# Hymba decoder layer on one Trainium2 core: the q, k, v projection shifted by 0.18 of a head pair against the attention that it runs beside, and the SSD half of the output projection begun later, with its evictions moved from VectorE to ScalarE and GpSimd

## The chip, the cores and the metric

One core of a Trainium2 chip runs the whole layer in one launch. The metric is the device time in microseconds (us). TensorE (PE) multiplies, with its weight loads on a queue of their own (PEld); VectorE (DVE), ScalarE (ACT) and GpSimd (POOL) do everything else; SyncE (SP) issues almost all DMAs, in one queue.

## The reference, cut to what matters

One layer on 1024 tokens of width 1024. The first sub-layer projects the normed input once, gives the first part to a Mamba-2 SSD mixer (16 heads) and the last 3072 columns to a stick-breaking attention (16 heads of 64), and projects both outputs back together:

```
q = rms_norm(q per head, q_norm_w); k = rms_norm(k per head, k_norm_w)
for each block of 128 queries:
    logits = q_blk @ k.T / 8                 # keys up to the block's end
    rem    = where(s < t, 1 - sigmoid(logits), 1)
    weights = where(s < t, sigmoid(logits) * (product of rem over the later keys), 0)
    out_blk = weights @ v
y = concat(norm(y_ssd), attention) ;  x1 = x + gate * (y @ w_out)
x2 = x1 + gate2 * swiglu(norm(x1))          # afterwards
```

The reference writes the product as an exponential of a cumulative sum of logarithms; the kernel forms it directly with a scan. `y_ssd` is normed in two groups of 512 columns, each with a factor of its own per token (`yr` in the kernel), which the kernel applies after the matmul to each group's product.

## The kernel before, in words

Every product is of float32 quality: both operands are split into a high and a low part, and `mm3` issues three matmuls (high·high, high·low, low·high) for each logical one.

Heads go in eight pairs, p = 0 to 7. The part of the program that the change touches is one list of "atoms": pieces of work, each with a time in units of one pair's attention. The list is sorted by that time, and the atoms are issued in this order. PE's instructions run in exactly this order; on the other engines a scheduler at build time sets the order. Four kinds of atoms matter:

- *Attention of pair p* (`Step`, lines 818 to 885), times p to p + 1: four steps i, each of two query blocks (0 and 1, 2 and 3, up to 7). A block n has (n + 1) x 128 keys. PE computes the logits `pl`, ACT takes two sigmoids of them (lines 843, 844), DVE runs the scan (line 848) and the multiplication (line 850) over the block's whole width for each of two heads, PE transposes the weights (`ptw`), ACT copies them out (line 865), and PE sums (`pa`). So the scans grow from 128 to 1024 columns in a pair and start again at 128.
- *Projection of pair p + 1*, beside the attention of pair p (`qkv_unit`, `unit_atoms`): four units u of 256 tokens, each 48 matmuls of 128x384 (`pp`), copied out by ACT (lines 777, 778). A norm follows: ACT squares, DVE reduces (line 785), GpSimd takes a reciprocal square root in small operations (lines 118 to 129, tile `rs_y`), DVE multiplies (line 790). Then PE transposes q and k (`pq`), ACT and DVE write their halves (lines 804 to 808). The attention of the next pair needs all this.
- *Weight pages.* The projection's weights of one pair are eight pages `wp` in nine buffers. During the last unit (u = 3), as each page is used for the last time, the page of the next pair is split into its place: high part by GpSimd (line 692), low part by DVE (line 694). I call the point between unit 3 of one pair and unit 0 of the next the border of the projection's pairs. With `SHIFT = 0` it coincides with the start of the next pair's attention.
- *The SSD half of the output projection* (`a0_block`), beside the attention of pair 7, which has no projection left to fill PE: eight blocks of 128 tokens, each with two groups of 12 matmuls of 128x384 (`poa`). Group 0 is evicted by ACT (line 984), group 1 by DVE (line 986), which adds group 0 in the same instruction. Two PSUM banks (pool `psp`) serve these accumulators. Input pages are loaded from DRAM (line 964) and split by ACT (968) and GpSimd (969). Line 671 sets when it begins (`A0T`) and how long a block takes (`A0D`). In the same stretch the weights of the next stage are loaded into seven buffers (line 1011) and split by ACT (1017) and DVE (1020). The next stage's matmuls are `po`.

Here pair 7's attention with all that lies beside it, up to the first `po`, is called the tail.

Of the kernel before, what the change touches and what calls it, by code (L numbers as in the profile page):

```python
# [10 lines left out]
AF = mybir.ActivationFunctionType  # L11
ALU = mybir.AluOpType
# [7 lines left out]
TB = S // P  # L20
# [9 lines left out]
def build(tc, t, dbg=None, stop=None):  # L30
    nc = tc.nc
# [635 lines left out]
    aw2 = ExitStack()  # L667
    apr = aw2.enter_context(tc.tile_pool(name="apr", bufs=1, side="right"))
    NP = H // 2
    SLOT0, CL, FL0, FL, FT0, LAG, LAGS, LAGQ, SHIFT, D0, E0, C0 = 300, 0.5, 0.0, 0.9, 0.12, 0.05, 0.1, 0.2, 0.0, 0.14, 0.0, -0.25  # L670
    A0T, A0D = 0.01, 0.14
    WD = -6
    WT = (7.18, 7.22, 7.26, 7.4, 7.7, 7.98, 7.99, 8.0)
    NPR, NWT = 3, 6
    CA = 3 * P
# [260 lines left out]
    def unit_atoms(p, u):  # L936

        g = qkv_unit(p, u)
        d = (NP - 1 + SHIFT) / (4 * (NP - 1))
        t0 = (4 * (p - 1) + u) * d  # L940
        if p == 0:
            d = D0
            t0 = (u - 4) * d + E0
        res = []
        for n in range(16):
            res.append((t0 + d * n / 16, lambda: next(g, None)))
            if u == 3 and p + 1 == NP and n < KT:
                res.append((t0 + d * (2 * n + WD) / 16, lambda n=n: qkv_load(NP, n)))
                res.append((t0 + d * (2 * n + 1) / 16 + 1e-6, lambda n=n: qkv_split(NP, n)))
            if u == 3 and p + 1 < NP:  # L950
                res.append((t0 + d * n / 16 + 1e-6, lambda n=n: qkv_weight(p + 1, n)))
        res.append((t0 + d + LAGS, lambda: next(g, None)))
        res.append((t0 + d + LAGQ, lambda: next(g, None), "unit"))
        return res


    x1 = [None] * TB
    y_pages, y_hl, x1_pages = [], {}, []

    def a0_load(i):  # L960
        if not y_pages:
            y_pages.extend(page("y_page").rearrange("p (k c) -> p k c", c=P) for _ in range(8))
            x1_pages.extend(apool.tile([P, D], F32, tag="page", name="x1") for _ in range(TB))
        dma(out=f32(y_pages[3 * (i & 1)]), in_=yssd_s[i])
# [7 lines left out]
    def a0_block(i):  # L972
        hi, lo = y_hl[i]
        x1[i] = x1_pages[i]
        xo = x1[i][:, 0:CA]
        for g in range(NG):
            po = psp.tile([P, 512], F32, tag="pp", name="poa")[:, 0:CA]
            for k in range(4 * g, 4 * g + 4):
                w = w_pages[NP, k]
                mm3(po, hi[:, k], lo[:, k], w[:, 0], w[:, 1], k == 4 * g, k == 4 * g + 3)  # L980
                if k % 4 < 3:
                    yield
            if g == 0:
                nc.scalar.activation(xo, po, AF.Copy, scale=yr[:, i:i + 1])
            else:
                nc.vector.scalar_tensor_tensor(out=xo, in0=po, scalar=yr[:, TB + i:TB + i + 1], in1=xo,
                                               op0=ALU.mult, op1=ALU.add)
            yield

    def a0_atoms():  # L990
        t0 = NP - 1 + A0T
        res = [(t0 - 0.01, lambda: a0_load(0)), (t0 - 0.01, lambda: a0_load(1)), (t0 - 0.005, lambda: a0_split(0))]
        for i in range(TB):
            t = t0 + i * A0D
            if i + 1 < TB:
                res.append((t + 0.1 * A0D, lambda i=i: a0_split(i + 1)))
            if i + 2 < TB:
                res.append((t + 0.2 * A0D, lambda i=i: a0_load(i + 2)))
            g = a0_block(i)
            for n in range(8):  # L1000
                res.append((t + A0D * n / 8, lambda g=g: next(g, None)))
        return res
# [22 lines left out]
    yr = rsqrt(NG * TB, yssq, 1.0 / 512, "yn", nc.gpsimd)  # L1025
# [427 lines left out]
    po = None  # L1453
# [45 lines left out]
```

## Time and profile before

| | us |
|---|---|
| time, median of 3 runs (lowest, highest) | 1788.65 (1782.85, 1790.51) |
| the profiled execution: its time, its span | 1781.2, 1779.5 |
| PE busy in the span | 1692.4 (95%) |
| DVE busy | 1190.8 (67%) |
| ACT busy | 839.9 (47%) |
| GpSimd busy | 298.0 (17%) |

The attention phase with the work beside it runs from about 402 to 947 us of the span. Of the page, in 40 slices of 44.5 us each, in tenths:

```
PE   3999999999999999999879999899999999999999
DVE  5597795757676676676786666976676666644541
PEclk9999999999999999999889999999999999999999
```

A digit is the busy share of a slice, in the third line the clock that TensorE was granted. The slices 9 to 20 (counted from 0) hold the attention phase: PE is at 9 tenths throughout, DVE at 6 to 8; only the last two (845 to 934 us) fall to 8 and 7 on PE, with a clock of 8 tenths: the tail.

### The profile page before, as it was taken

How to read it: one execution, taken by the hardware profiler on the slowest of the kernel's cores; microseconds unless marked ns; L12 is line 12 of the kernel's file. 1: busy time of each engine (PE TensorE's matmuls, PEld its weight loads, DVE VectorE, ACT ScalarE, POOL GpSimd, SP SyncE). 2: the span in 40 equal slices, each digit the busy share in tenths (PEclk: the TensorE clock that was granted, in tenths of full speed). 3: DMA queues.
4: the chain of work that ended last, by engine and by line, in shares of the span. 5: the costliest groups of instructions: out<-in, count | busy, mean ns of one | idle time of the engine just before them, and what ended most of it. 6: DMA issues, size and time to landing. Idle time of an engine off the chain costs nothing.

```text
span 1779.5 us, 24616 instructions
## 1 busy us (share of the span) xinstructions
PE 1692.4 (95%) x9025; PEld 1401.2 (79%) x9025; DVE 1190.8 (67%) x1789; ACT 839.9 (47%) x1651; POOL 298.0 (17%) x630
## 2 busy tenths in 40 slices
PE   3999999999999999999879999899999999999999
PEld 2777777798788778778669888688888888788887
DVE  5597795757676676676786666976676666644541
ACT  6545562556666566667564345533332332423220
POOL 2410001033422431432522710000000000000000
PEclk9999999999999999999889999999999999999999
DMA  8366355311101110111314433532332222844621
GB/s 282 117 220 209 119 181 155 105 54 43 42 21 34 45 37 16 45 42 30 118 38 143 160 119 111 149 125 78 95 113 77 87 86 72 274 158 148 236 89 48
DMA packets 175792, 192.17 MB, mean 108 GB/s; under 512 B 11560, under 2 KB 126516, under 8 KB 175671
## 3 DMA queue, kind: packets, MB, share of 16 engines
q1 hardware_dynamic: 174582, 190.07, 33.7%
q8 instruction: 71, 1.16, 0.3%
q10 hardware_dynamic: 1088, 0.52, 0.1%
q14 instruction: 51, 0.41, 0.1%
HBM read 155.88 MB, written 34.67 MB: 107 GB/s over the span
## 4 chain that ended last, share of the span: by engine, by line
PE 64%; DVE 14%; DMA 7%; issue 6%; ACT 4%; POOL 4%; SPq 1%; DVEq 0%; POOLq 0%; ACTq 0%
PE pdn L50 13%; PE pX L50 10%; PE pY L50 6%; PE pp L50 6%; PE po L50 6%; PE pZ L50 6%; PE px L50 5%; DVE pr L848 3%; PE pz L50 3%; PE pa L50 2%; DVE be L850 2%; PE pyd L50 2%; PE pl L50 1%; PE ptw L53 1%; DMA adaraw<-in_w_ada_dram 1%
## 5 line engine op out<-in xcount | busy, mean ns | idle before, releaser
L50 PE MATMUL pp<-wp,hh 128*128 128x384 f32 x1024 | 284.9, 356 | 14.5 <-DVE wp L694 13.3
L50 PE MATMUL pdn<-dw,ah 128*128 128x512 f32 x704 | 217.0, 389 | 1.5 <-DVE t L1334 1.5
L50 PEld LDWEIGHTS pp<-wp,hh 128*128 128x128 f32 x1024 | 173.5, 189 | 33.8 <-DVE wp L694 17.5
L848 DVE TENSOR_TENSOR_SCAN pr<-pr,idz 128x256 f32<-128x256 f32 (+7 forms) x128 | 175.5, 1392 | 29.2 <-ACT pr L843 29.2
L50 PE MATMUL pp<-wp,hl 128*128 128x384 f32 x512 | 172.7, 337 | 0.0
L50 PEld LDWEIGHTS pdn<-dw,ah 128*128 128x128 f32 x704 | 132.1, 188 | 29.4 <-DVE t L1334 2.0
L50 PE MATMUL pdn<-dw,al 128*128 128x512 f32 x352 | 136.9, 389 | 0.0
L843 ACT ACTIVATE pr<-pl 128x384 f32<-128x384 f32 (+3 forms) x192 | 97.2, 506 | 61.5 <-PE pl L50 44.9
L865 ACT COPY wt<-ptw 128x512 f32<-128x512 f32 (+1 forms) x160 | 88.8, 569 | 67.4 <-PE ptw L53 67.2
L1434 ACT CAST ah<-araw 128x1024 fp32r<-128x1024 f32 x44 | 46.4, 1055 | 142.9 <-PE pdn L50 130.6
L1298 ACT CAST wl<-s 128x512 fp32r<-128x512 f32 x88 | 54.8, 623 | 123.5 <-PE pX L50 42.0
L65 DVE TENSOR_TENSOR wl<-s,wl 128x512 fp32r<-128x512 f32 x88 | 60.6, 691 | 67.0 <-ACT wl L1298 66.3
L850 DVE TENSOR_TENSOR be<-be,pr 128x256 f32<-128x256 f32 (+7 forms) x128 | 101.8, 817 | 4.8
L790 DVE TENSOR_TENSOR qkraw<-qkraw,rs_y 128x256 f32<-128x256 f32 x64 | 34.3, 559 | 99.2 <-POOL rs_y L129 99.2
L844 ACT ACTIVATE be<-pl 128x384 f32<-128x384 f32 (+3 forms) x192 | 98.0, 510 | 0.1
L50 PEld LDWEIGHTS pp<-wp,hl 128*128 128x128 f32 x512 | 96.2, 188 | 0.2 <-issue 0.2
L65 DVE TENSOR_TENSOR al<-araw,ah 128x1024 fp32r<-128x1024 f32 x44 | 53.7, 1223 | 59.7 <-ACT ah L1434 59.6
L53 PE MATMUL ptw<-ident,be 128*128 128x128 f32 x576 | 90.6, 276 | 1.1 <-DVE be L850 1.1
L50 PE MATMUL pz<-zw,hh 128*128 128x512 f32 x256 | 89.5, 417 | 0.0
L1298 ACT CAST wl<-raw 128x512 fp32r<-128x512 f32 x62 | 38.5, 622 | 98.9 <-PE pY L50 41.6
L50 PE MATMUL pa<-wt,qv 128*64 128x256 f32 (+1 forms) x640 | 77.5, 374 | 4.0 <-ACT qv L778 3.8
L50 PE MATMUL po<-wb,yhi 128*128 128x512 f32 x256 | 80.9, 397 | 0.0
(373 smaller groups left out, 4055.2 us busy)
## 6 DMA issues: line engine op xcount, KB each, us to landing
araw<-a_s SPq DMA_DIRECT2D x44, 512.0 KB, 3.5
adaraw<-in_w_ada_dram SPq DMA_DIRECT2D x64, 256.0 KB, 3.4
wraw<-in_w_in_dram SPq DMA_DIRECT2D x64, 192.0 KB, 3.1
raw<-in_w_gate_dram SPq DMA_DIRECT2D x46, 256.0 KB, 3.0
raw<-in_w_up_dram SPq DMA_DIRECT2D x44, 256.0 KB, 3.2
draw<-in_w_down_dram SPq DMA_DIRECT2D x44, 256.0 KB, 3.4
ada_raw<-in_w_ada_dram SPq DMA_DIRECT2D x16, 512.0 KB, 5.9
seg<-csT_s SPq DMA_DIRECT2D x32, 256.0 KB, 3.1
```

The costliest lines, as they stand in the source:

```text
L50: link(nc.tensor.matmul(out, lhsT, rhs, start=start, stop=stop, skip_group_check=more))
L53: link(nc.tensor.transpose(out=out, in_=in_, identity=identity or ident))
L65: return nc.vector.tensor_tensor(out=lo, in0=src, in1=f32(hi), op=ALU.subtract)
L790: inst = nc.vector.tensor_tensor(out=r4[:, t2], in0=r4[:, t2], in1=r[:, t2].unsqueeze(2).to_broadcast([P, 4, HD]), op=ALU.mult)
L843: nc.scalar.activation(pr[:, c0:c1], pl[:, 0:c1 - c0], AF.Sigmoid, scale=-1.0)
L844: nc.scalar.activation(be[:, c0:c1], pl[:, 0:c1 - c0], AF.Sigmoid)
L848: nc.vector.tensor_tensor_scan(out=rev, data0=rev, data1=idz[:, S - n:][:, ::-1], initial=0.0, op0=ALU.mult, op1=ALU.max)
L850: nc.vector.tensor_tensor(out=be[:, 0:n], in0=be[:, 0:n], in1=pr[:, 1:n + 1], op=ALU.mult)
L865: nc.scalar.copy(wt[:, 0:m], pt[:, 0:m])
L1298: nc.scalar.copy(w[:, 0], src)
L1434: nc.scalar.copy(ah, raw)
```

## The change

`SHIFT` goes from 0 to 0.18: the projection of every pair is issued 0.18 of a pair later against the attention. Each unit lasts 0.25 of a pair, as before; only the first unit of pair 1 is stretched over the first 0.43 of pair 0's attention. The SSD half of the output projection begins at 7.27 instead of 7.01 and takes 0.1 instead of 0.14 per block; its first loads and its first split go to 7.18. Its second group is now evicted by ACT into the second 384 columns of the same page, `part`, and GpSimd adds that to the first.

```
-    ... SHIFT, D0, E0, C0 = ..., 0.0, 0.14, 0.0, -0.25
-    A0T, A0D = 0.01, 0.14
+    ... SHIFT, D0, E0, C0 = ..., 0.18, 0.14, 0.0, -0.25
+    A0T, A0D = 0.27, 0.1
 def unit_atoms(p, u):
-        d = (NP - 1 + SHIFT) / (4 * (NP - 1))
-        t0 = (4 * (p - 1) + u) * d
+        d = 0.25
+        t0 = SHIFT + (4 * (p - 1) + u) * d
+        if p == 1 and u == 0:
+            d, t0 = d + SHIFT, 0.0
 def a0_block(i):
-            if g == 0:
-                nc.scalar.activation(xo, po, AF.Copy, scale=yr[:, i:i + 1])
-            else:
-                nc.vector.scalar_tensor_tensor(out=xo, in0=po, scalar=yr[:, TB + i:TB + i + 1], in1=xo,
-                                               op0=ALU.mult, op1=ALU.add)
+            part = (xo, x1[i][:, CA:2 * CA])[g]
+            nc.scalar.activation(part, po, AF.Copy, scale=yr[:, g * TB + i:g * TB + i + 1])
+            if g:
+                nc.gpsimd.tensor_tensor(out=xo, in0=xo, in1=part, op=ALU.add)
 def a0_atoms():
-        t0 = NP - 1 + A0T
-        res = [(t0 - 0.01, lambda: a0_load(0)), (t0 - 0.01, lambda: a0_load(1)), (t0 - 0.005, lambda: a0_split(0))]
+        t0, t1 = NP - 1 + A0T, NP - 1 + SHIFT + 1e-3
+        res = [(t1, lambda: a0_load(0)), (t1, lambda: a0_load(1)), (t1 + 1e-3, lambda: a0_split(0))]
```

Later lines of the changed kernel have numbers higher by two (964 is 966, 1011 is 1013, 1017 is 1019); the evictions are lines 987 (ACT) and 989 (GpSimd).

Counted in PE's order: every pair from 1 to 6 keeps its 192 projection matmuls, pair 0 has 159 instead of 192 and four transposes fewer, and 33 matmuls and four transposes stand in pair 7 in their place.

On DVE, at the border of the projection's pairs, this is what stood before between the two halves of the widest block (`pr`, `be` are the scan and the multiplication, `wp` the low parts of the new pages, `qkred` the norm's reduction and `rs_y` the multiplication by the root):

```order
L785 TENSOR_REDUCE qkred<-sqv 128x8
L790 TENSOR_TENSOR qkraw<-qkraw,rs_y 128x256 x2
L848 SCALAR_TENSOR_TENSOR pr_3167<-pr_3167,idz 128x1024
L848 SCALAR_TENSOR_TENSOR pr_3165<-pr_3165,idz 128x1024
L850 TENSOR_TENSOR be<-be,pr_3167 128x1024
L850 TENSOR_TENSOR be<-be,pr_3165 128x1024
L694 SCALAR_TENSOR_TENSOR wp<-wraw,wp 128x384 x5
L808 SCALAR_TENSOR_TENSOR qv<-qkraw,cols_79,qv 128x256
L808 SCALAR_TENSOR_TENSOR kp<-qkraw,cols_79,kp 128x256
L694 SCALAR_TENSOR_TENSOR wp<-wraw,wp 128x384
```

And now on DVE, the same stretch and what follows it:

```order
L785 TENSOR_REDUCE qkred<-sqv 128x8
L790 TENSOR_TENSOR qkraw<-qkraw,rs_y 128x256 x2
L848 SCALAR_TENSOR_TENSOR pr_3165<-pr_3165,idz 128x1024
L848 SCALAR_TENSOR_TENSOR pr_3166<-pr_3166,idz 128x1024
L850 TENSOR_TENSOR be<-be,pr_3165 128x1024
L850 TENSOR_TENSOR be<-be,pr_3166 128x1024
L808 SCALAR_TENSOR_TENSOR qv<-qkraw,cols_79,qv 128x256
L808 SCALAR_TENSOR_TENSOR kp<-qkraw,cols_79,kp 128x256
L785 TENSOR_REDUCE qkred<-sqv 128x8
L790 TENSOR_TENSOR qkraw<-qkraw,rs_y 128x256 x2
L848 SCALAR_TENSOR_TENSOR pr_3167<-pr_3167,idz 128x128
L850 TENSOR_TENSOR be<-be,pr_3167 128x128
```

The new pages' splits have moved from behind the scans of 1024 columns to behind those of 128 columns of the next pair; a reduction with its multiplication stands there now. In a whole pair, all four reductions are now followed directly by the multiplication that needs GpSimd's root of it; before, two of four were not.

On DVE in the tail, before, the evictions of group 1 (`poa`) stood among the scans and multiplications of wide blocks:

```order
L986 SCALAR_TENSOR_TENSOR x_8945<-poa,rs_y,x_8945 128x384
L848 SCALAR_TENSOR_TENSOR pr_3165<-pr_3165,idz 128x640
L848 SCALAR_TENSOR_TENSOR pr_3166<-pr_3166,idz 128x640
L850 TENSOR_TENSOR be<-be,pr_3165 128x640
L850 TENSOR_TENSOR be<-be,pr_3166 128x640
L848 SCALAR_TENSOR_TENSOR pr_3167<-pr_3167,idz 128x768
L848 SCALAR_TENSOR_TENSOR pr_3165<-pr_3165,idz 128x768
L850 TENSOR_TENSOR be<-be,pr_3167 128x768
L850 TENSOR_TENSOR be<-be,pr_3165 128x768
L986 SCALAR_TENSOR_TENSOR x_8946<-poa,rs_y,x_8946 128x384
```

On ACT in the tail, now, the evictions of blocks 1 and 2 (both groups, line 987) stand among splits of the next stage's weights (`wa`):

```order
L1019 ACTIVATE wa<-waraw,cols_78 128x640
L987 ACTIVATE x_9009<-poa,rs_y 128x384
L1019 ACTIVATE wa<-waraw,cols_78 128x640
L865 COPY wt<-ptw 128x512
L1019 ACTIVATE wa<-waraw,cols_78 128x640
L987 ACTIVATE x_9009<-poa,rs_y 128x384
L1019 ACTIVATE wa<-waraw,cols_78 128x640
L865 COPY wt<-ptw 128x512
L987 ACTIVATE x_9010<-poa,rs_y 128x384
```

The evictions that waited among DVE's scans are gone from DVE; ACT's second to fourth ones now have a `wa` split ahead of each. On SP, the loads which these splits need are issued in this order now (`y_page` are the input pages of the SSD half, in the order of its blocks, `ysb_s` the attention's output):

```order
L883 DMA ysb_s<-yth 128x2x128
L966 DMA y_page<-yssd_s 128x1024 x2
L883 DMA ysb_s<-yth 128x2x128
L966 DMA y_page<-yssd_s 128x1024 x2
L1013 DMA waraw<-in_w_out_dram 128x640 x7
L966 DMA y_page<-yssd_s 128x1024 x2
L1013 DMA waraw<-in_w_out_dram 128x640
```

The seven weight loads stand behind the pages of blocks 4 and 5, as they did before; the pages themselves are loaded later.

## Rows read from the trace of the kernel before

**Rows 1.** Waits of PE, 310 to 960 us: total us, times, longest.
```profile
PE pp L50 <- DVE wp L694: 13.3, 11, 2.1
PE poa L50 <- DVE x L986: 8.7, 2, 7.8
PE poa L50 <- POOL y_page L969: 5.4, 1, 5.4
PE pa L50 <- ACT qv L778: 3.8, 6, 0.6
```
**Rows 2.** One pair's window: length, busy PE PEld DVE ACT POOL, PE's clock, DMA.
```profile
527.00:592.00 65.00, 62.15 (x435) 52.71 (x433) 45.74 (x61) 42.41 (x104) 20.89 (x65) 1.00 0.13 33
```
**Rows 3.** PE's timeline around a border: start, busy us, ..., [wait <-releaser].
```profile
490.82 1.15 PE L50 MATMUL pl<-kp,qv 64*128 64x256 f32 x12
...
505.57 1.49 PE L50 MATMUL pl<-kp,qv 64*128 64x384 f32 x12
509.13 0.60 PE L53 MATMUL pq<-ident,qkraw 128*128 128x128 f32 x4
...
522.70 0.60 PE L53 MATMUL pq<-ident,qkraw 128*128 128x128 f32 x4
...
529.96 0.44 PE L50 MATMUL pp<-wp,hh 128*128 128x384 f32 x1 [2.03 <-DVE wp L694]
```
**Rows 4.** The chain of waits, a run of projection matmuls: start, us.
```profile
388.96 4.70 PE pp L50 x27
```
**Rows 5.** DVE's timeline of the same pair.
```profile
493.12 2.87 DVE L848 TENSOR_TENSOR_SCAN pr<-pr,idz 128x640 f32<-128x640 f32 x2 [0.70 <-ACT pr L843]
497.36 0.48 DVE L808 SCALAR_TENSOR_TENSOR qv<-qkraw,cols,qv 128x256 fp32r<-128x256 f32 x1
498.15 0.68 DVE L785 TENSOR_REDUCE qkred<-sqv 128x8 f32<-128x512 f32 x1
...
502.84 0.76 DVE L790 TENSOR_TENSOR qkraw<-qkraw,rs_y 128x256 f32<-128x256 f32 x2 [4.01 <-POOL rs_y L129]
...
509.27 3.94 DVE L848 TENSOR_TENSOR_SCAN pr<-pr,idz 128x896 f32<-128x896 f32 x2 [0.64 <-ACT pr L843]
...
515.12 0.48 DVE L808 SCALAR_TENSOR_TENSOR qv<-qkraw,cols,qv 128x256 fp32r<-128x256 f32 x1
...
529.36 2.42 DVE L694 SCALAR_TENSOR_TENSOR wp<-wraw,wp 128x384 fp32r<-128x384 f32 x5
```
**Rows 6.** DVE's waits for the norm's root, 527 to 592 us: total, times, longest.
```profile
DVE qkraw L790 <- POOL rs_y L129: 13.2, 4, 4.0
```
**Rows 7.** PE in pair 0's attention.
```profile
412.85 0.99 PE L53 MATMUL pq<-ident,qkraw 128*128 128x128 f32 x4 [1.44 <-DVE qkraw L790]
```
**Rows 8.** PE in the tail.
```profile
859.35 1.65 PE L50 MATMUL poa<-wp,y_page 128*128 128x384 f32 x4 [5.39 <-POOL y_page L969]
...
910.27 1.33 PE L50 MATMUL poa<-wp,y_page 128*128 128x384 f32 x3 [7.82 <-DVE x L986]
...
946.79 3.93 PE L50 MATMUL po<-wa,y_page 128*128 128x320 f32 x25
```
**Rows 9.** Windows of the tail, columns as in rows 2.
```profile
853.00:947.00 94.00, 76.31 (x483) 61.88 (x484) 68.59 (x68) 51.39 (x107) 28.37 (x25) 0.87 0.24 75
858.00:864.00 6.00, 4.65 (x18) 4.46 (x19) 5.89 (x8) 0.90 (x2) 2.96 (x3) 0.54 0.36 109
```
**Rows 10.** Evictions of the SSD half by ACT: shortest, median, longest ns.
```profile
L984 ACT ACTIVATE x<-poa,rs_y x8: 581/652/678, 864.3 to 936.0; 128x384 f32<-128x384 f32 x8
```
**Rows 11.** GpSimd's timeline: splits ahead of the attention phase, and in the tail.
```profile
399.42 3.23 POOL L692 TENSOR_SCALAR wp<-wraw 128x384 fp32r<-128x384 f32 x5
...
847.08 9.61 POOL L692 TENSOR_SCALAR wp<-wraw,cols 128x384 fp32r<-128x384 f32 x5
856.66 2.63 POOL L969 TENSOR_TENSOR y_page<-y_page 128x1024 fp32r<-128x1024 f32 x1
```
**Rows 12.** DMA issues of 780 to 960 us: KB each, us to landing.
```profile
y_page<-yssd_s SPq DMA_DIRECT2D x8, 512.0 KB, 3.6
waraw<-in_w_out_dram SPq DMA_DIRECT2D x8, 320.0 KB, 4.2
```

More of the change, by code (lines that the diff above doesn't have):

```diff
@@ L669, in build @@
     NP = H // 2
-    SLOT0, CL, FL0, FL, FT0, LAG, LAGS, LAGQ, SHIFT, D0, E0, C0 = 300, 0.5, 0.0, 0.9, 0.12, 0.05, 0.1, 0.2, 0.0, 0.14, 0.0, -0.25
-    A0T, A0D = 0.01, 0.14
+    SLOT0, CL, FL0, FL, FT0, LAG, LAGS, LAGQ, SHIFT, D0, E0, C0 = 300, 0.5, 0.0, 0.9, 0.12, 0.05, 0.1, 0.2, 0.18, 0.14, 0.0, -0.25
+    A0T, A0D = 0.27, 0.1
     WD = -6
```

## The prediction

> **What bounds the kernel now.** I read the waits of PE first. In the attention phase PE is busy nearly all the time, so its waits are what a reordering can give back, and they lie in two places [rows 1]: at the borders PE waits for DVE's low parts of the new pages (13.3 us in 11 waits) and for ACT's copy of v (3.8 us in six); in the tail it waits for DVE's eviction (8.7 us, one wait of 7.8) and for one GpSimd split (5.4 us).
>
> Next the window of one steady pair: 65.0 us, in which PE is busy 62.15 at clock 1.00, so 2.85 us are idle; DVE is busy 45.74, ACT 42.41, GpSimd 20.89 [rows 2]. No other engine's sum comes near PE's; only the order on them can make PE wait. The timeline names the place: the first matmul on a new page begins at 529.96 after 2.03 us of waiting [rows 3], and the five splits it needs start on DVE at 529.36 [rows 5], since in DVE's order they stand behind both scans and both multiplications of 1024 columns.
>
> Last the tail: 94.00 us with PE busy 76.31 at a mean clock of 0.87 [rows 9]. Scaled, 76.3 x 0.87 = 66.4 us would be left at full clock without waits. So 27.6 us are lost there: 14.1 in the two waits above, the rest to short waits and the low clock.
>
> All terms below are against the profiled execution, 1781.2 us, 7.45 under the median of the runs; I subtract their sum from the median.
>
> **Border of the pairs.** The splits now stand on DVE behind the scans of 128 columns of the next pair, which are short, and PE comes to the first new page only some 11 us into that pair. Adding up DVE's rows in the new order, the first four splits are done 0 to 2 us before PE asks. I take the 2.2 us of the page waits per border as gone, and the 0.6 of the copy of v, as PE has other work between unit 3 and the next use of its bank: 2.85 in all, six times.
>
> What is late next: the norm. Each of a pair's four reductions is now followed directly by the multiplication that waits for GpSimd's root. DVE waits four times, 13.2 us in all, 4.0 at most [rows 6]; four full waits make 16.0. That is DVE's idle time, but the transposes `pq` stand behind it on PE. For the unit beside query block 6: before, `pl` starts at 505.57 and `pq` at 522.70, 17.13 us later [rows 3]. The new order has 15 projection matmuls, 6 transposes of weights and 4 `pq` fewer between them. At 4.70/27 = 0.174 us a matmul [rows 4] that is 2.6, and some 0.9 for the transposes, so PE comes after 13.6. DVE needs from `pl`: 3.1 to 3.7 to its scan (505.57 to 509.27, 0.64 of it waiting), 5.85 for scans and multiplications (to 515.12), 4.69 from reduction to multiplication (498.15 to 502.84) and 0.76 [rows 5], 14.4 to 15.0. PE waits 0.8 to 1.4; I take 1.0. For the unit beside block 4: 18.31 us from 490.82 to 509.13 [rows 3], from which the new order takes 15 matmuls, a group of logits (about 1.5, the row at 505.57), eight sums and some transposes, 6 to 7 together: 11.3 to 12.3. DVE needs 2.30 to its scan, 4.24 to 497.36, 4.69 and 0.76, 12.0 [rows 5]. PE waits 0 to 0.7; I take 0.4. The other two units' transposes have more PE work ahead of them. So a pair gains 2.85 - 1.4 = 1.45, six times **8.7 us**; bounds 0 (the waits eat all) and 17.1.
>
> **Pair 0.** 33 matmuls leave it: 33 x 0.174 = 5.7, and four transposes 0.4. Before its third `pq` at 412.85 PE already waits 1.44 for DVE [rows 7]; there 15 matmuls are missing ahead, so PE comes 2.6 earlier and waits that much longer, and 0.7 more goes to new `pq` waits as above. **Gain 2.8**; bounds 2.0 and 6.1 (no wait grows). The same work comes back in the tail.
>
> **Tail.** Work at full clock: 66.4 + 33 x 0.174 + 0.4 = 72.5. The wait of 7.82 [rows 8] goes, as DVE's scans no longer hold the second group. The wait of 5.39 [rows 8] came from a split that GpSimd started at 856.66, behind five page splits that took 9.61 from 847.08 [rows 11]; now the 33 matmuls of unit 3 lie beside these. I leave 1 us for it and 1 for `pq`.
>
> What is late next: ACT. It holds all 16 evictions, and in its order the second group of block 1 and the first of block 2 stand behind `wa` splits, whose loads stand on SP behind the load of page 5, which must wait for split 3 to give up its buffer. I follow this chain from pair 7's first logits as 0; where no row is named the times are estimates, the work in the new order added up at the paces above. The last unit's matmuls end near 11, its root on GpSimd at 17 to 18.4, then split 1 (2.63 [rows 11]) at 19.8 to 21.2; load 3 may start then and lands 3.6 later [rows 12], its cast by ACT and split 3 (2.63) end at 27 to 29; load 5 is issued, and a weight load behind it lands 2.7 to 4.2 later [rows 12], at 31 to 34; ACT's `wa` split (0.9, an estimate from the 0.652 eviction of 384 columns [rows 10] for 640) and the eviction end at 33 to 35. PE wants that bank for block 2 at 28.2 to 29.4. It waits 2.8 to 6; I take 4.5, and 1 for block 1's second group.
>
> Clock: behind the 5.39 us wait the granted clock was 0.54 for the next 6 us, the lower level of 1.2 GHz; a border's wait of 2.03 left 1.00 in its window [rows 2, 3, 8, 9]. A wait of 4.5 lies between; I take 3 us for the clock, the loss of 6 us at half speed. The tail becomes 72.5 + 2 + 5.5 + 3 = 83, **a gain of 11**; bounds 0 (ACT stalls as DVE did) and 19 (only short waits are left).
>
> The Trainium skill ("TensorE: Matmul & The Clock Gate", Part 1: The HAM clock gate) says that PE drops to half its rate when it has not been busy of late, which the row after the 5.39 us wait agrees with. If 4.5 us don't make it fall, the tail is 80 and the sum 3 us better.
>
> GpSimd's eight adds of 128x384: bounded by its page splits of that size, 3.23/5 = 0.65 and 9.61/5 = 1.92 [rows 11], 5 to 15 us in all. They are hidden: `xo` is next read when the next stage's result is added. DVE loses eight evictions, ACT gains eight at 0.65 [rows 10], costed by their order above. That GpSimd slows beside DVE's scans is seen in the two rows (threefold). The Trainium skill ("SBUF — State Buffer", SBUF: two separate sides) says that DVE and GpSimd share a port pair which one of them holds for a whole instruction, the other blocked meanwhile: that speaks against moving additions to GpSimd. By it DVE could lose 5 to 15 us over the tail's 94, but DVE, busy 68.6 of these [rows 9], no longer holds PE's banks, so the sum would stay.
>
> **Sum:** -2.8 - 8.7 - 11 = -22.5; the profile would show 1758.7, the median **1766**.
>
> **The rivals.**
>
> A. All is covered: no new wait on `pq`, and ACT's chain arrives in time. For it: the chain and the `pq` gaps are margins of 1 to 5 us on estimates of 12 to 30. Against: three of them point the same way. -2.8 - 17.1 - 20 = -40: 1748.
>
> B. The border gives nothing: the multiplication's waits of 1.4 in my sum are 2.85, as the bounds of 1.4 and 0.7 with one more late unit would make them. For it: the 4.0 us waits of DVE are certain. The tail gains alone: -2.8 - 11 = -13.8: 1775.
>
> C. The tail gives nothing: ACT, which takes sigmoids and copies in the same order, holds two banks as long as DVE did (7.8). -2.8 - 8.7: 1777. With B as well (E): -2.8: 1786.
>
> D. Slower. DVE's four waits of 4.0 become the bound: if PE comes to `pq` of both late units with nothing else to issue, each holds it the full 4.0, as the order of PE lets nothing pass. A pair is then 62.15 + 8 = 70.2, 5.2 longer, six times 31; pair 0 and the tail give 13.8 back: 1788.65 + 31 - 14 = 1806. It decides once the two waits exceed 2.85 by more than 2.3 per pair (13.8/6). Against it: PE has 42 projection matmuls (7.3 us) ahead of each, so the waits computed above are 0 to 1.4.
>
> **How the numbers follow.** Forecast 0.50, A 0.15, B 0.15, C 0.08, E 0.07, D 0.05. The forecast's own range, from 0.4 to 2.0 gained per pair and a tail of 78 to 87, is 1757 to 1775. The range 1752 to 1785 holds it, B, C and the nearer part of A, and leaves out most of A (toward 1748), E and D. About 8.9 us (0.5%) is what a measurement of this kernel can tell from no change: below 1779.7 is faster. Forecast, A and B lie wholly or almost there, C mostly; E is the same, with the edges of B and C: faster 0.82, same 0.13, slower 0.05.
>
> **What would show it.** Right: no waits of PE for the page splits' DVE line, border to border 63 to 64 us; new waits for line 790 of 0.3 to 1.4 in every pair; pair 0 shorter by 2 to 4; in the tail no wait for DVE, one of 3 to 6 for ACT's eviction behind a `wa` split, the length from pair 7's first logits to `po` 78 to 87. Wrong: page waits of 2 us still at the borders (then DVE's new place for them is late as well); waits of 3 or more for line 790 (D); several waits for ACT's evictions that sum to over 10 (C); a tail near 74 (A).

## The result, and the profile after

The changed kernel took 1767.64 us (median of 4 runs, 1765.23 to 1769.38) against 1785.75 for the kernel before (4 runs), a ratio of 0.9895 with a 95% interval of 0.9876 to 0.9913. The prediction was 1766 in a range of 1752 to 1785. The gain is 18.1 us between these medians; 22.5 was forecast. The total came out close to the forecast, its parts less so, and the parts are what follows.

The profiled execution has a span of 1765.5 us against 1779.5, only 14.0 less. The difference to 18.1 lies ahead of the change: the first logits of pair 0 start at 406.26 us, 3.9 later than before. Six profiles of kernels with PE's order alike up to that point (this one and e3, e4, e5, e6 and e8 below) have that start at 401.3 to 408.0, so it scatters by run. From there on I compare by PE's own landmarks, the first logits (`pl`) of each pair and the first `po`:

| stretch on PE | before | after | forecast for the difference | measured |
|---|---|---|---|---|
| pair 0 | 58.98 | 57.13 | -2.8 | -1.9 |
| pairs 1 to 6, mean of one | 65.26 | 63.34 | -1.45 | -1.92 |
| pairs 1 to 6, sum | 391.56 | 380.04 | -8.7 | -11.5 |
| tail | 93.92 | 89.82 | -11 | -4.1 |
| all of these | 544.46 | 526.99 | -22.5 | -17.5 |

The waits of PE in the attention phase of the changed kernel (total us, times, longest), to be read against [rows 1]:

```profile
PE pq L53 <- DVE qkraw L790: 13.2, 15, 4.8
PE poa L50 <- ACT x L987: 3.9, 2, 3.5
PE ptw L53 <- DVE be L850: 2.5, 2, 2.4
PE poa L50 <- POOL y_page L971: 2.0, 1, 2.0
```

The page waits (13.3 us) and the waits for the copy of v (3.8) are gone, DVE's evictions (8.7) too. In their place PE waits for the multiplication by the root, fifteen times (13.2 us; two times and 3.5 us before). One pair's window, which answers to [rows 2], says how much a border was worth: 63.23 instead of 65.00 with the same work.

```profile
526.63:589.86 63.23, 62.32 (x435) 52.65 (x434) 45.98 (x61) 42.22 (x104) 16.20 (x64) 1.00 0.13 34
```

PE's and DVE's timelines of the pair ahead of it answer to [rows 3, 5]: start, busy us, then the instruction, and in brackets what ended a wait.

```profile
489.73 1.15 PE L50 MATMUL pl<-kp,qv 64*128 64x256 f32 x12
...
501.83 0.79 PE L53 MATMUL pq<-ident,qkraw 128*128 128x128 f32 x4 [0.47 <-DVE qkraw L790]
...
505.27 1.50 PE L50 MATMUL pl<-kp,qv 64*128 64x384 f32 x12
...
519.35 0.79 PE L53 MATMUL pq<-ident,qkraw 128*128 128x128 f32 x4 [0.43 <-DVE qkraw L790]
```
```profile
508.28 3.94 DVE L848 TENSOR_TENSOR_SCAN pr<-pr,idz 128x896 f32<-128x896 f32 x2 [0.42 <-ACT pr L843]
...
514.12 0.68 DVE L785 TENSOR_REDUCE qkred<-sqv 128x8 f32<-128x512 f32 x1
518.77 0.76 DVE L790 TENSOR_TENSOR qkraw<-qkraw,rs_y 128x256 f32<-128x256 f32 x2 [3.98 <-POOL rs_y L129]
...
534.66 2.27 DVE L694 SCALAR_TENSOR_TENSOR wp<-wraw,wp 128x384 fp32r<-128x384 f32 x4
```

The last row is the pages' splits behind the scans of 128 columns of the next pair, 8.0 us after its first logits at 526.63; PE lists no wait for them in any pair. The rows above it are the new wait: the transposes come 14.08 us after their block's logits, 0.43 of which PE waited, so PE arrived after 13.65.

Pair 0, to be read against [rows 7], and the tail, against [rows 8, 9]:

```profile
417.20 1.35 PE L53 MATMUL pq<-ident,qkraw 128*128 128x128 f32 x4 [4.77 <-DVE qkraw L790]
```
```profile
867.35 0.69 PE L50 MATMUL poa<-wp,y_page 128*128 128x384 f32 x1 [2.03 <-POOL y_page L971]
867.84 0.41 PE L53 MATMUL pq<-ident,qkraw 128*128 128x128 f32 x1
870.12 0.90 PE L53 MATMUL pq<-ident,qkraw 128*128 128x128 f32 x3 [1.87 <-DVE qkraw L790]
...
882.80 1.32 PE L50 MATMUL poa<-wp,y_page 128*128 128x384 f32 x6 [3.52 <-ACT x L987]
...
921.00 0.55 PE L53 MATMUL ptw<-ident,be 128*128 128x128 f32 x3 [2.36 <-DVE be L850]
```
```profile
865.00:867.00 2.00, 0.32 (x2) 0.00 (x0) 1.97 (x1) 0.00 (x0) 2.00 (x1) 1.00 0.00 0
867.00:869.00 2.00, 0.90 (x2) 0.47 (x2) 2.00 (x2) 0.00 (x0) 2.00 (x2) 0.60 0.38 72
...
867.00:875.00 8.00, 5.78 (x27) 4.43 (x29) 7.60 (x8) 3.29 (x6) 3.59 (x3) 0.57 0.50 149
...
923.00:925.00 2.00, 2.00 (x9) 1.56 (x10) 0.93 (x3) 0.75 (x2) 0.00 (x0) 0.50 0.46 176
...
843.43:933.25 89.82, 79.52 (x521) 66.73 (x519) 69.07 (x64) 59.02 (x123) 45.81 (x50) 0.94 0.27 89
```

PE is idle for 10.3 us of the tail (89.82 - 79.52). Its clock falls twice. From 867 to 869 us the mean is 0.60, so it went from 1.00 to 0.50 near 867.4, as the wait of 2.03 ended and before the one of 1.87 began (868.25). The second fall stands behind the wait of 2.36. The wait of 3.52 for ACT was forecast as 4.5. Its cause is the forecast one: the eviction on ACT stands behind a split that waited for its load.

```profile
881.46 0.83 ACT L1019 ACTIVATE wa<-waraw,cols 128x640 fp32r<-128x640 f32 x1 [1.93 <-DMA waraw<-in_w_out_dram]
882.19 0.56 ACT L987 ACTIVATE x<-poa,rs_y 128x384 f32<-128x384 f32 x1
```

What the forecast did not count stands on DVE and GpSimd from 865 and from 898 us. First GpSimd's, then DVE's timeline:

```profile
864.95 4.83 POOL L971 TENSOR_TENSOR y_page<-y_page 128x1024 fp32r<-128x1024 f32 x2
...
902.07 7.34 POOL L971 TENSOR_TENSOR y_page<-y_page 128x1024 fp32r<-128x1024 f32 x2
```
```profile
865.03 5.03 DVE L790 TENSOR_TENSOR qkraw<-qkraw,rs_y 128x256 f32<-128x256 f32 x2 [4.00 <-POOL rs_y L129]
...
898.22 5.78 DVE L848 TENSOR_TENSOR_SCAN pr<-pr,idz 128x896 f32<-128x896 f32 x2 [1.04 <-ACT pr L843]
903.92 6.43 DVE L850 TENSOR_TENSOR be<-be,pr 128x896 f32<-128x896 f32 x2
...
914.59 5.24 DVE L848 TENSOR_TENSOR_SCAN pr<-pr,idz 128x1024 f32<-128x1024 f32 x2
```

The two multiplications by the root, 0.76 in a steady pair, take 5.03 beside two subtractions of the input pages on GpSimd. The transposes behind them (867.84 and 870.12) are released one by one. The kernel before had this already: its tail shows the same pair of multiplications (x2: busy us, mean ns) and PE's wait behind it.

```profile
L790 DVE TENSOR_TENSOR qkraw<-qkraw,rs_y 128x256 f32<-128x256 f32 x2 | 5.1, 2577 | 3.0 <-POOL rs_y L129 3.0
```
```profile
PE pq L53 <- DVE qkraw L790: 2.1, 1, 2.1
```

### The profile page after: what moved, and what is told of

Read it like the earlier page. It is cut to its first block, busy times and chain, and to the rows that moved or that the text cites. A ratio compares the mean times of both kernels' runs of the same rounds, so it can differ in the third digit from the quotient of the medians.

```text
span 1765.5 us, 24607 instructions
## 1 busy us (share of the span) xinstructions
PE 1693.4 (96%) x9025; PEld 1401.9 (79%) x9025; DVE 1190.4 (67%) x1781; ACT 841.9 (48%) x1659; POOL 276.3 (16%) x638
## 4 chain that ended last, share of the span: by engine, by line
PE 69%; DVE 13%; issue 6%; DMA 5%; POOL 4%; ACT 3%; SPq 0%; DVEq 0%; ACTq 0%; POOLq 0%
PE pdn L50 13%; PE pX L50 10%; PE pp L50 9%; PE pY L50 6%; PE pZ L50 6%; PE po L50 4%; PE px L50 4%; PE pa L50 3%; PE pz L50 3%; PE ptw L53 2%; PE pl L50 2%; DVE be L850 2%; PE pyd L50 2%; DVE pr L848 2%; PE pq L53 1%
## 5 line engine op out<-in xcount | busy, mean ns | idle before, releaser
L50 PEld LDWEIGHTS pp<-wp,hh 128*128 128x128 f32 x1024 | 172.2, 189 | 15.0 <-issue 11.8
L50 PE MATMUL px<-hh,xhi 128*128 128x512 f32 x192 | 79.4, 413 | 1.7 <-ACT hh L329 1.2
```

Source lines behind the costliest of these rows:

```text
L50: link(nc.tensor.matmul(out, lhsT, rhs, start=start, stop=stop, skip_group_check=more))
```

## The experiments

My theory after the result: the border's gain is the shift's alone; the eviction's move matters in the tail only; and the tail's forecast missed because GpSimd's two-input operations hold DVE up, and the clock falls behind the waits which that makes. Rivals: the evictor's change is worth nothing; ACT alone keeps the tail long. All times are medians, ratios against the kernel before on the same chip, with 95% intervals; the stretches are read from each run's one profile. The edits of e3, e4, e5 and e6 do not touch pair 0, and it reads 57.1 to 58.1 in these and the changed kernel, so a difference of a microsecond in a stretch tells little.

| kernel | us | ratio | pair 0 | pair 1 to 6, mean | tail |
|---|---|---|---|---|---|
| changed kernel | 1767.64 | 0.9895 [0.9876, 0.9913] | 57.13 | 63.34 | 89.82 |
| e1 eviction undone | 1768.87 | 0.9906 [0.9891, 0.9921] | 57.57 | 63.43 | 91.27 |
| e2 eviction alone | 1775.12 | 0.9945 [0.9929, 0.9962] | 59.33 | 65.75 | 84.98 |
| e3 later weight splits | 1760.77 | 0.9868 [0.9853, 0.9883] | 57.42 | 63.40 | 85.87 |
| e4 subtractions on DVE | 1762.71 | 0.9870 [0.9854, 0.9887] | 58.10 | 63.42 | 85.10 |
| e5 additions on DVE | 1765.39 | 0.9883 [0.9852, 0.9913] | 57.99 | 63.32 | 87.46 |
| e6 e3 and e4 | 1760.61 | 0.9854 [0.9822, 0.9885] | 57.33 | 63.34 | 83.30 |
| e7 e6, later `pq` | 1756.20 | 0.9832 [0.9803, 0.9861] | 55.85 | 63.78 | 80.09 |
| e8 half the shift | 1796.75 | 1.0059 [1.0043, 1.0076] | 58.76 | 69.46 | 81.21 |
| e10 root on DVE | 1747.48 | 0.9793 [0.9777, 0.9810] | 54.25 | 61.78 | 84.41 |
| e11 e6, root on DVE | 1744.59 | 0.9772 [0.9758, 0.9787] | 55.30 | 61.77 | 78.97 |
| e12 e7, root on DVE | 1737.76 | 0.9729 [0.9715, 0.9744] | 53.34 | 61.65 | 76.72 |
| e13 e8, root on DVE | 1760.60 | 0.9868 [0.9845, 0.9891] | 54.19 | 65.34 | 78.22 |

**e1, the eviction undone.** In the changed kernel:

```
-            part = (xo, x1[i][:, CA:2 * CA])[g]
-            nc.scalar.activation(part, po, ...)
-            if g:
-                nc.gpsimd.tensor_tensor(out=xo, in0=xo, in1=part, op=ALU.add)
+            if g == 0:
+                nc.scalar.activation(xo, po, ...)
+            else:
+                nc.vector.scalar_tensor_tensor(out=xo, in0=po, ..., in1=xo, op0=ALU.mult, op1=ALU.add)
```

> The changed kernel with the second group's eviction undone: VectorE evicts it and adds the first group, as before; the shift and the later, shorter blocks stay. Theory (the border's gain is the shift's alone, the eviction is worth something only in the tail): pairs 1 to 6 stay at 63.1 to 63.9 us each; in the tail PE waits again for VectorE's eviction, 4 to 8 us, and the tail is 93 to 97 us instead of 89.8; about 1772. Rival (GpSimd's adds cost VectorE by the shared port as much as the evictions did): tail 88 to 91, the waits for the multiplication by the root and for the 1024-wide block shorter; about 1767.

The pairs stay, as both had it. The tail is 91.27, between the rival's 88 to 91 and the theory's 93 to 97. PE's waits for DVE's evictions are back, but small:

```profile
PE poa L50 <- DVE x L989: 5.6, 2, 3.1
```

The longest is 3.1 where it was 7.8. With the shift and the later blocks in place, the eviction's move is worth 1.5 us in the tail; by the ratios (0.9906 and 0.9895, their intervals overlapping) nothing that can be told. Half of the rival is true as well: PE does not wait for the 1024-wide block here.

**e2, the eviction alone** (the same lines in the kernel before, shift 0, blocks at 7.01).

> The kernel before with only the eviction changed (ScalarE evicts both groups, GpSimd adds); shift 0, blocks at 7.01 in steps of 0.14. Theory: pairs stay at 65.0 to 65.2; in the tail the wait of 7.8 us for VectorE goes and a part of it comes back as other waits; tail 86 to 91 instead of 93.9; 0.2 to 0.45% faster than before. Rival (the evictor's queue moves from VectorE to ScalarE and GpSimd's adds block VectorE): tail 92 to 96, no change.

The rival did not come, and the gain is above the theory's: the tail is 84.98, 8.9 us less (86 to 91 expected), the time 0.55% less (0.2 to 0.45), and PE's waits for DVE's evictions are replaced by shorter ones for ACT's.

```profile
PE pp L50 <- DVE wp L694: 13.0, 10, 2.1
PE poa L50 <- ACT x L984: 5.4, 2, 2.8
```

So either part alone takes about 9 us from the tail: e1's 91.27 holds 33 matmuls and four transposes moved from pair 0, 6.1 us by the prediction's count, and 91.27 - 6.1 = 85.2 stands against 84.98 and 93.92. Together they give 89.82 - 6.1 = 83.7, a gain of 10.2 and not of 17.6.

The waits alone nearly add up. PE's idle time in the tail is 17.7 us before, 11.8 in e1, 13.5 in e2 and 10.3 with both parts: 5.9 and 4.2 less alone, 7.4 together, or 9.8 but for the wait of 2.4 for the 1024-wide block, which neither part alone has. The rest is the clock: taking 75.3 us (e12, below) as the work at full clock, and 69.2 where the 6.1 are not in it, PE is busy longer than that by 7.0 before, 4.1 in e1, 2.3 in e2 and 4.2 with both. So each part by itself also takes away clock loss (2.9 and 4.7), and together they take away no more of it (2.8) than one.

Three of e2's pairs (1, 2 and 6) are longer than before, at a lower mean clock, though their page wait is the same 2.0 to 2.1 us:

```profile
459.75:525.98 66.23, 63.46 (x434) 54.26 (x432) 45.79 (x61) 42.39 (x104) 21.05 (x65) 0.97 0.12 33
...
591.98:657.01 65.03, 62.16 (x434) 52.70 (x433) 45.67 (x61) 42.39 (x104) 21.04 (x65) 1.00 0.13 34
```

The clock sometimes falls behind a border's wait, and costs some 1 us when it does. No pair of the kernel before shows it in its profile (1.00 in all six); where it happens, the border's gain is larger than in the profiles compared here.

**e3, the weight splits later.**

```
-    WT = (7.18, 7.22, 7.26, 7.4, 7.7, 7.98, 7.99, 8.0)
+    WT = (7.5, 7.52, 7.54, 7.6, 7.75, 7.98, 7.99, 8.0)
```

> The changed kernel with the next stage's first weight splits issued later (their times 7.50 to 7.60 instead of 7.18 to 7.40), so that on ScalarE the eviction of block 1's first group stands ahead of them and only one split stands ahead of its second; the loads stand where they stood. Theory (ScalarE's eviction waits behind a split whose load is late): the 3.5 us wait of PE for ScalarE's eviction shrinks to 0.5 to 1.5, the tail is 2 to 3 us shorter than 89.8, if nothing else ends later. Rival (VectorE, late with the 1024-wide block, sets the tail's end): the wait shrinks, but the wait of 2.4 for the 1024-wide block grows by as much; tail 89 to 91.

ACT's eviction of block 1 no longer waits for a load; PE's waits for ACT are 3.2 us, 1.5 at most. The tail is 4.0 shorter, more than the 2 to 3 of the theory, as the wait for the 1024-wide block went from 2.4 to 0.3; the rival's exchange did not come.

**e4, the subtractions on DVE.**

```
-        after(nc.gpsimd.tensor_tensor(out=lo, in0=raw, in1=f32(hi), op=ALU.subtract), chain["pool"])
+        nc.vector.tensor_tensor(out=lo, in0=raw, in1=f32(hi), op=ALU.subtract)
```

> The changed kernel with the low parts of the SSD half's eight input pages formed by VectorE (one subtraction of 128x1024 each) instead of GpSimd. Theory (GpSimd's two-input operations hold VectorE up while they run: 5.03 us for two multiplications of 0.76 beside two of them, 4.75 and 6.43 for the multiplications of the 768 and 896 blocks): each subtraction takes 1.2 to 1.4 on VectorE, 10 to 11 in all, and gives back as much or more; the two multiplications take 0.8 again, PE's wait for them in the tail (1.9) and for the 1024-wide block (2.4) shrink to under 1 each, the clock does not fall after them; tail 83 to 86. Rival (VectorE is slow there for another reason, or its queue is full): the durations stay, VectorE is 10 us busier and the 1024-wide block later; tail 90 to 98.

The theory held for the durations and the length of the tail. DVE's timeline, to be read against 5.03 and 6.43 above, and the tail's window:

```profile
864.37 0.76 DVE L790 TENSOR_TENSOR qkraw<-qkraw,rs_y 128x256 f32<-128x256 f32 x2 [4.02 <-POOL rs_y L129]
...
900.64 2.84 DVE L850 TENSOR_TENSOR be<-be,pr 128x896 f32<-128x896 f32 x2
```
```profile
842.51:927.61 85.10, 78.76 (x521) 66.90 (x519) 61.74 (x72) 58.53 (x123) 26.00 (x42) 0.96 0.28 93
```

DVE has eight operations more and is busy for 61.74 instead of 69.07 us. Being blocked showed as busy time. The tail is 4.7 shorter. Two things limit what this shows. The clock still fell once (0.96 over the tail), now behind a new wait of 2.4 us for ACT's copies (`wt`). And the edit also takes the splits out of GpSimd's queue, where one stood behind the root; PE's wait of 2.0 for a split is gone with it, so the 4.7 are not the hold-up alone.

**e5, the additions on DVE.**

```
-                nc.gpsimd.tensor_tensor(out=xo, in0=xo, in1=part, op=ALU.add)
+                nc.vector.tensor_tensor(out=xo, in0=xo, in1=part, op=ALU.add)
```

> The changed kernel with the eight additions of the second group's part done by VectorE instead of GpSimd; ScalarE still evicts both groups. Theory (a two-input operation of GpSimd holds up VectorE's operations that read two inputs; the additions are a smaller part of this than the eight subtractions of the input pages): VectorE gets 8 x 0.5 = 4 us more work, the multiplications of the 768 to 1024 blocks lose part of their excess, the two multiplications by the root stay at 5.0 beside the subtractions; tail 87 to 90 against 89.8. Rival (the additions are what holds VectorE up): the multiplications are back at 2.6, 2.8 and 2.3 us and the tail is 84 to 86. Other rival (no hold-up by them at all): VectorE later by 4 us, tail 91 to 94.

87.46, inside the theory's 87 to 90: taking the additions that the change gave GpSimd off it saves 2.4 us of the tail, taking off the subtractions that were there already saves 4.7. The multiplication of the 896 block still takes 6.4 us for two, and that of the 768 block 6.2, against the theory. What went back are the scans of 896 and 1024 columns, 3.9 and 4.5 us for two instead of 5.8 and 5.2, and with them PE's wait for the 1024-wide block. (Count | busy us, mean ns.)

```profile
L850 DVE TENSOR_TENSOR be<-be,pr 128x896 f32<-128x896 f32 x2 | 6.4, 3242 | 0.0
...
L848 DVE TENSOR_TENSOR_SCAN pr<-pr,idz 128x896 f32<-128x896 f32 x2 | 3.9, 2001 | 0.0
```

e1, in which GpSimd adds nothing either, has the same: 6.4 for the multiplications, 3.9 and 4.5 for the scans, no wait.

**e6, e3 and e4 together.**

> The two edits together: the eight subtractions on VectorE and the weight splits later. Theory (they end different waits: the first that for the multiplications and the split, the second that for ScalarE behind a late load): the tail is 82 to 83.5, against 85.1 and 85.9 with one of them; about 1759. Rival (both shorten the same chain, as the two parts of the change did): 84.5 to 85.5.

83.30: the theory's value, 1.8 and 2.6 us under e4 and e3, whose own gains were 4.7 and 4.0; they share about 2 us. In the whole time e6 cannot be told from e3.

**e7, the transposes later as well.**

```
-    ... LAG, LAGS, LAGQ, SHIFT, ... = ..., 0.05, 0.1, 0.2, 0.18, ...
+    ... LAG, LAGS, LAGQ, SHIFT, ... = ..., 0.05, 0.1, 0.23, 0.18, ...
```

> As the last one, and the transposes of q and k 0.03 of a pair later (0.23 instead of 0.20 behind their unit), which puts 6 more projection matmuls and 2 to 3 transposes of weights ahead of them on PE in every pair. Theory (PE is early at these transposes by 0.4 to 0.6, twice a pair, because VectorE waits 4 us for GpSimd's root): 1.3 us more work ahead ends both waits; pairs 62.2 to 62.6 instead of 63.3, 5 to 6 us over the six, pair 0 1 to 1.5 shorter; about 1753. Rival (what comes later makes the next pair's first logits or the border late): pairs stay at 63 to 63.5, with the wait elsewhere.

Half a miss. One of the two waits in each pair went, the other stayed at 0.4, and PE's busy time rose by 0.7, so the pairs did not gain (the rival); pair 0 and the tail did (1.5 and 3.2). Here is one pair:

```profile
521.05:584.51 63.46, 63.00 (x435) 52.98 (x433) 46.00 (x61) 41.29 (x104) 16.01 (x64) 1.00 0.13 34
```

Why PE is busy 0.7 us longer with the same matmuls was not settled; e12 below has the same later transposes and does not show it.

**e8, half the shift.** In the changed kernel:

```
-    ... SHIFT, ... = ..., 0.18, ...
-    A0T, A0D = 0.27, 0.1
+    ... SHIFT, ... = ..., 0.09, ...
+    A0T, A0D = 0.18, 0.1
```

> The changed kernel with half the shift: 0.09 instead of 0.18, and the SSD half's start at 7.18 instead of 7.27. On VectorE the new pages' splits stand directly behind the 1024-wide block and one reduction, as in the kernel before nearly; PE comes to the first new page 0.09 x 65 = 5.9 us into the pair instead of at once. Theory (what counts at the border is only that PE comes later than these splits, which start 2.9 us into the pair): no wait for pages, and the transposes of q and k stand elsewhere; pairs 62.2 to 63.3. Rival (the splits must leave the place behind the 1024-wide block): waits for pages of 0.5 to 2 at each border, pairs 63.5 to 65.

Both were wrong on the time: the page waits are gone, as the theory had it, yet a pair takes 69.46 and the kernel is 0.6% slower than before. PE's and DVE's timelines behind a pair's first logits at 536.22, and the windows of the pair and of 2 us behind the wait:

```profile
542.33 0.30 PE L53 MATMUL pq<-ident,qkraw 128*128 128x128 f32 x1 [3.88 <-DVE qkraw L790]
```
```profile
538.55 0.56 DVE L694 SCALAR_TENSOR_TENSOR wp<-wraw,wp 128x384 fp32r<-128x384 f32 x1 [2.77 <-POOL wp L692]
...
541.47 1.36 DVE L790 TENSOR_TENSOR qkraw<-qkraw,rs_y 128x256 f32<-128x256 f32 x2
```
```profile
536.22:605.14 68.92, 64.59 (x434) 54.73 (x432) 45.38 (x60) 42.29 (x104) 16.27 (x65) 0.98 0.12 31
...
544.00:546.00 2.00, 2.00 (x9) 1.90 (x8) 1.60 (x4) 1.72 (x4) 0.79 (x1) 0.50 0.09 15
```

This is a wait of the kind of the prediction's rival D, at another setting: the transposes stand six projection matmuls behind the first logits, with nothing else for PE to issue. It is not the root's alone, since on DVE three page splits, which wait for GpSimd's high parts, stand ahead of the multiplication (e13). Of the 5.7 us that this pair takes over the changed kernel's 63.2, 3.4 are idle time (4.33 here, 0.91 there); the busy time is 2.3 longer, with the clock at 0.50 behind the wait.

**e10, the root on DVE.**

```
-        r = rsqrt(8, red, 1.0 / HD, "qk", nc.gpsimd).rearrange(...)
+        r = rsqrt(8, red, 1.0 / HD, "qk").rearrange(...)
```

> The changed kernel with the norm's reciprocal root (8 values a row) computed by VectorE, in 11 small operations, instead of by GpSimd in 14; everything else as it was. Theory (PE's two waits of 0.4 to 0.5 in each pair, 4.8 in pair 0 and 1.9 in the tail are VectorE's 4.0 us wait for this root, handed on): VectorE needs 11 x 0.2 = 2.2 to 2.5 us where it waited 4.0; both waits of a pair vanish and a pair is 62.3 to 62.8 instead of 63.2; pair 0 loses 2 to 4 us of its 57.1 and the tail 1 to 3 of its 89.8; about 1759. Rival (VectorE is busy enough that 2.4 us more for each unit come back as later scans): pairs 63 to 64, no gain.

The waits vanish from the pairs and the tail, one of 3.1 us stays in pair 0, and the gain is 20 us by the medians (17.7 in the stretches of the table) where 9 was expected. DVE's timeline (the second row is the first of the root's eleven operations) and a pair:

```profile
506.49 0.68 DVE L785 TENSOR_REDUCE qkred<-sqv 128x8 f32<-128x512 f32 x1
507.20 0.17 DVE L118 TENSOR_SCALAR rs_v<-qkred 128x8 f32<-128x8 f32 x1
...
509.42 0.76 DVE L790 TENSOR_TENSOR qkraw<-qkraw,rs_y 128x256 f32<-128x256 f32 x2
```
```profile
518.22:579.87 61.65, 61.65 (x434) 52.77 (x432) 53.64 (x105) 41.91 (x104) 4.88 (x8) 1.00 0.13 35
```

From the reduction's start to the multiplication 2.93 us instead of 4.65, on an engine that has the time: PE is busy without a gap. A pair gains 1.6 though only 0.9 of waits was listed; PE's busy time falls by 0.7 too, 0.4 of it in the transposes that had waited. Pair 0 gains 2.9 and the tail 5.4.

**e11 and e12, the root on DVE in e6 and in e7.**

> Subtractions on VectorE and weight splits later (83.3 us in the tail before this edit), and the root on VectorE as well. Theory: pairs 62.3 to 62.8, tail 80 to 83; about 1753. Rival (VectorE now holds scans, roots and subtractions in the tail, and becomes late there): tail 84 to 88, about 1757.

> The last one with the transposes of q and k 0.03 of a pair later too. Theory: nothing waits for the multiplication by the root any more except in pair 0, where that wait falls by 1.5 to 2; pairs 62.3 to 63.0, pair 0 about 54, tail 79 to 81; about 1750. Rival (the later transposes cost PE something without a wait: its busy time in a pair was 63.0 instead of 62.3 with them): pairs stay at 63.0 to 63.5; about 1755.

The tails are 78.97 and 76.72, both better than expected: DVE did not become late. In e12 a pair is 61.45 us with PE busy throughout, so the later transposes by themselves cost PE nothing. e12 is the best version, 1737.76 us, 2.7% below the kernel before. Its tail:

```profile
825.57:902.29 76.72, 75.32 (x521) 64.00 (x519) 64.65 (x92) 58.59 (x123) 17.34 (x13) 1.00 0.33 104
```

1.4 us are idle there and the clock is 1.00, so 75.3 is what the prediction estimated as 72.5, the tail's work at full clock.

**e13, half the shift with the root on DVE.**

> The kernel with half the shift (0.09), and the root on VectorE. There PE waits 3.9 us for the multiplication by the root just behind every pair's first logits and its clock falls after it, so that a pair takes 68.6 to 70 us. VectorE's order is now reduction, root, three page splits, multiplication. Theory (the wait is made of GpSimd's root and of the page splits that stand ahead of the multiplication and wait for GpSimd's high parts, which stood behind the root on GpSimd): without the root GpSimd splits earlier, the multiplication comes 1.5 to 3 us earlier, the wait is 1 to 2.4, the clock stays; pairs 64 to 66.5. Rival (the wait is only the late end of the 1024-wide block on VectorE): wait 3 to 4 and pairs 68 to 70 as before.

The theory held for the wait: the longest is 2.2 instead of 3.9, the pairs take 65.34, the kernel is 1.3% faster than before. The clock did not stay in all of them: pairs 1 and 4, at 0.97, take 66.1 and 66.0, pairs 2, 3 and 5, at 1.00, 64.5. A pair is still 2.0 us longer than with the shift of 0.18 and the root on GpSimd, and 3.6 longer than in e10.

## Why the prediction was right, and where it was not

**The border: right in mechanism, 2.8 us too small.** The page waits and the copy's wait went, 2.85 a pair, and the multiplication by the root took their place, as said. For the unit beside block 4 PE came 11.6 us after its logits (11.3 to 12.3 forecast) and waited 0.47 (0.4). For the one beside block 6 it came after 13.65 (13.6) and waited 0.43, not 1.0: DVE's chain from the logits was the over-sized term: 3.01 to the scan, 5.84 for scans and multiplications, 4.65 to the root's multiplication and 0.58 to the first transpose, 14.1, instead of 14.4 to 15.0. The first of these was taken as up to 3.7 and the last as 0.76. e10 shows that the root decides over these waits: with it on DVE, 1.7 us shorter from reduction to multiplication (2.93 for 4.65), they are gone.

**Pair 0: right in kind, 1 us too large.** The wait of 4.77 was forecast as 1.44 + 2.6 = 4.0. The clock, 0.97 over that pair, was not in the sum: PE's busy time fell by 4.9 us (56.6 to 51.7), not by the 6.1 of the work that left.

**The tail: the step that was mis-sized.** Forecast 83, measured 89.8, which is outside the 78 to 87 that the prediction gave as a sign of being right; nor did "no wait for DVE" come true there. Of its terms, the waits for the split (2.0, with 1 forecast), for the root (1.9, with 1) and for ACT (3.9, with 5.5) came to 7.8 against 7.5. Missing were the wait for the 1024-wide block (2.4, with nothing forecast) and the work at full clock, 75.3 by e12 instead of 72.5. The clock took the rest: 79.5 busy less 75.3 is 4.2, with 3 forecast. Together 83.0 + 0.3 + 2.5 (with 0.2 for another block) + 2.8 + 1.2 = 89.8.

The largest of these, 2.8, is a row read wrongly. The prediction scaled PE's busy 76.3 us by 0.87, the mean clock of the whole window, but for part of the time at the lower clock PE was waiting and not busy. Busy time times clock, summed over half-microsecond slices of the same trace, is 68.8 and not 66.4. With the 6.1 us of work that moved there it is 74.9, and the same sum over the changed kernel's tail is 75.1.

The size of ACT's wait is in part luck. PE wanted the bank 35.9 us after pair 7's first logits (28.2 to 29.4 forecast) and the eviction ended after 39.3 (33 to 35), both late by some 4 to 8 us.

Behind most of the rest is one sentence of the prediction: that DVE, if it loses time beside GpSimd, no longer holds up PE. It failed at both ends of the tail. DVE's multiplication by the root was stretched from 0.76 to 5.03, and PE waited 1.9 behind it; the kernel before had this too (5.1 and 2.1), so the change did not bring it, but the forecast left only 1 us for it. The clock's first fall is not its work, as it came before, at the end of the wait for the split. At the other end the 1024-wide block came late, a wait of 2.4 and the second fall of the clock: the multiplications of the 768 and 896 blocks took 4.8 and 6.4 us for two beside the subtractions, and the scans of 896 and 1024 columns were stretched besides. e4 takes the subtractions away: the durations of the three multiplications are 0.8, 2.6 and 2.8, and the tail is 4.7 us shorter. e1 and e5 take the additions away: the scans go back and the wait for the block is gone, though the multiplications stay long. So it took both. The Trainium skill ("SBUF — State Buffer", SBUF: two separate sides), which the prediction weighed and set aside, says that the two engines share a port pair that one holds for a whole instruction; the traces agree (5.03 against 0.76), and it should have been a term. The additions, the part of it that the change brought, account for 2.4 (e5).

**The overlap that was not forecast.** The prediction gave the 7.82 us wait to the eviction's move. By e1 the shift with the later blocks shortens it to 3.1 at most (5.6 in all, of 8.7) without that move, and by e2 the move alone leaves 2.8 for ACT's evictions in its place. The sum does not change by this, but the credit does.

**The total: in part luck.** By the stretches 17.5 us were gained of the 22.5 forecast: the tail fell short by 6.9 and pair 0 by 0.9, and the border gave 2.8 more, an error the other way. That 1766 is so close to 1767.64 has another reason too: it was counted from the median of 1788.65 that the kernel before then had, 2.9 above the 1785.75 of the result.

**The rivals.** A (1748) missed by the waits above. B, C and E did not come, B and C each had one true half: new waits on `pq`, and ACT as a blocked evictor, by 3.5 and not 7.8 (e3). D did not come at 0.18 but is real: at 0.09 a 3.88 us wait of that kind makes the kernel 0.6% slower than before (e8). The distance that PE's work keeps it behind DVE's chain decides, and at 0.18 it was short by less than half a microsecond.

## What to carry to other kernels

When a shift takes a wait away, look at what the engine waits for next, and count how much work stands ahead of it in the new order: 42 matmuls ahead left PE half a microsecond too early, six left it 3.9 us too early, and 6 us a pair longer. A chain of tiny dependent operations on an otherwise idle engine (14 on GpSimd, 4.0 us) is still latency on the path of whoever waits for it; moved to a busier but quicker engine it gave as much again (17.7 us in the stretches above) as the change studied here (17.5). Two edits that each took 9 us off one stretch took 10 together, as part of what they remove, the loss of clock, is the same, and together they made a new wait: try each alone. And do not scale an engine's busy time by the mean clock of a window in which it also waits: here that was 2.4 us too little.

## What the runs showed of the hardware

A two-input operation of GpSimd stretched DVE's multiplications and scans beside it, and the profile counts the stretched time as busy: the same pair of multiplications took 0.76 and 5.03 us, two scans of 1024 columns 4.46 (e5) and 5.24 beside additions, and DVE's busy time fell by 7.3 us when eight operations were added to it (e4). The Trainium skill ("SBUF — State Buffer", SBUF: two separate sides) says that the one holds the port pair and the other is blocked; that this falls into the busy column is what the traces add.

The clock behind a wait of PE: after 3.88 us of waiting in e8 it was 0.50, the 1.2 GHz level, from 544 to 546 us, some 2 us behind the wait's end. In the changed kernel's tail it fell as a wait of 2.03 us ended and again behind one of 2.36. After the 3.52 us for ACT's eviction there it stayed at 2.4 GHz, while behind 3.58 us of the same wait in e5 it was 0.50 from 883 to 885 us. The changed kernel's rows:

```profile
879.00:883.00 4.00, 0.48 (x3) 0.20 (x2) 3.87 (x6) 2.04 (x5) 0.00 (x0) 1.00 0.92 311
883.00:887.00 4.00, 4.00 (x29) 3.47 (x29) 4.00 (x7) 3.90 (x7) 1.35 (x1) 1.00 0.87 291
```

And the 2.0 to 2.1 us at a border left it at 1.00 in all pairs of before, but not in three of e2's six. The length of one wait does not tell by itself whether the clock falls.
